# Softmax with a relative position bias: the first reload waits for one store instead of one and a half, and the engines' code stands without a block around it

## The chip, the cores and the metric

The kernel runs on one core of a Trainium2 chip. The metric is the device time of one execution in microseconds (us), the median of several executions of one build. The granted clock was 1.00 in every run, and no TensorE work is done.

Each profile covers one execution. Its "span" is 1.6 to 2.4 us shorter than the time that the metric gives for the same execution.

## The reference

```python
B, H, S = (2, 8, 2112)          # logits (B, H, S, S), rel_bias (H, 33), float32
rel = pos[:, None] - pos[None, :]
bias = rel_bias[:, np.clip(rel, -16, 16) + 16]
logits = logits + bias[None]
logits = logits - logits.max(axis=-1, keepdims=True)
exp = np.exp(logits)
return exp / exp.sum(axis=-1, keepdims=True)
```

285 MB are read once and 285 MB are written once.

## The kernel before

The 33,792 rows are spread over 128 partitions. A tile is R = 4 rows on each partition, 4224 KB. There are N = 66 tiles and BUFS = 6 buffers. VectorE adds the bias in place, ScalarE does the exponential with the row sums, VectorE scales. SyncE issues the stores and two short first loads; GpSimd issues the other loads. A reload of a buffer waits until the store out of it has landed. In the code, `take` waits until a semaphore (a counter that engines and transfers raise) has reached a value, and subtracts that value; `half` is the semaphore of the first half of the second store. The `nc.Block` holds one stream of instructions for each engine.

```python
    section = ctx.enter_context(tc.tile_critical(name="rows"))        # line 76
    ...
    def take(eng, sem, v):
        eng.wait_ge(sem, v).then_inc(sem, -v)

    def load(eng, u, start):
        eng.dma_start(out=L[u][:], in_=rows(logits, start)).then_inc(loaded[u], 16)

    def store(eng, u, start):
        take(eng, scaled, 1)
        eng.dma_start(out=rows(out, start), in_=L[u][:]).then_inc(stored[u], 16)

    def reload(eng, u, start):
        take(eng, stored[u], 16)
        load(eng, u, start)
    ...
    with nc.Block() as block:                                         # line 217

        @block.sync
        def _(eng):
            ...                                                       # first rows
            store(eng, 0, 0)
            take(eng, scaled, 1)
            for r0, r1, sem in ((0, R // 2, half), (R // 2, R, stored[1])):
                eng.dma_start(
                    out=rows(out, R + r0, (r1 - r0) * S), in_=L[1][:, r0 * S : r1 * S]
                ).then_inc(sem, 16)
            for n in range(2, BUFS):
                store(eng, n, n * R)
            passes(eng, BUFS, lambda u, start, loads: store(eng, u, start))
            for n in range(BUFS):
                take(eng, stored[n], 16)

        @block.gpsimd
        def _(eng):
            ...                                                       # first loads
            take(eng, half, 16)
            passes(eng, BUFS, lambda u, start, loads: reload(eng, u, start))
        ...                                                           # scalar, vector
```

The softmax here doesn't subtract the row's maximum and nothing guards it: scores larger than these inputs give would overflow.

Of the kernel before, what the change touches and what calls it, by code (L numbers as in the profile page):

```python
# [7 lines left out]
FP32 = mybir.dt.float32  # L8
INT32 = mybir.dt.int32
EXP = mybir.ActivationFunctionType.Exp  # L10
# [4 lines left out]
def kernel(  # L15
# [16 lines left out]





    nc = tc.nc
    P = 128
    B, H, S, S2 = logits.shape
# [4 lines left out]
    T = S // Q  # L44
    assert Q * B * H == P and T * Q == S and T % W == 0
    M = T // W
    R = 4
    PARTS = [(0, 2), (2, R)]
    BUFS = 6
    N = T // R  # L50
    assert N * R == T and N % BUFS == 0
    FW = S + T - 1
    NB = (FW - 2 * MR) // W
    assert NB * W + 2 * MR == FW
# [5 lines left out]
    one = const.tile([P, 1], FP32, tag="one", name="one")  # L60
    L = [const.tile([P, RS], FP32, tag=f"L{u}", name=f"L{u}") for u in range(BUFS)]
# [3 lines left out]
    qi, mm, qm, eq, lt, gt, rest = (  # L65
        L[BUFS - 1][:, NB * m : NB * (m + 1)] for m in range(7)
    )
    qi = qi.bitcast(INT32)
    mm = mm.bitcast(INT32)

    def rows(t, start, run=RS):
        return bass.AP(
            tensor=t.tensor, offset=t.offset + start * S, ap=[[T * S, P], [1, run]]
        )

    section = ctx.enter_context(tc.tile_critical(name="rows"))
    loaded = [nc.alloc_semaphore(f"loaded{u}") for u in range(BUFS)]
    stored = [nc.alloc_semaphore(f"stored{u}") for u in range(BUFS)]
    table = nc.alloc_semaphore("table")
    blocks_ready = nc.alloc_semaphore("blocks_ready")  # L80
    strip = nc.alloc_semaphore("strip")
    first = nc.alloc_semaphore("first")
    half = nc.alloc_semaphore("half")
    made = nc.alloc_semaphore("made")
    added = nc.alloc_semaphore("added")
    summed = nc.alloc_semaphore("summed")
# [1 line left out]
    scaled = nc.alloc_semaphore("scaled")  # L88
# [14 lines that stand above are left out]
# [16 lines left out]
    def exps(eng, u):  # L119
        for r0, r1 in PARTS:  # L120
            take(eng, added, 1)
            for i in range(r0, r1):
                x = L[u][:, i * S : (i + 1) * S]
                e = eng.activation(out=x, in_=x, func=EXP, accum_out=tot[u][:, i : i + 1])  # L124
            e.then_inc(summed, 1)

    def vec(eng, u, start, loads):
        eng.wait_ge(loaded[u], loads)
        for r0, r1 in PARTS:
            add(eng, u, r0, r1, start)  # L130
        for r0, r1 in PARTS:
            take(eng, summed, 1)
            t = tot[u][:, r0:r1]
            eng.reciprocal(out=t, in_=t).then_inc(inverted, 1)  # L134
            take(eng, inverted, 1)
            for i in range(r0, r1):
                x = L[u][:, i * S : (i + 1) * S]
                e = eng.tensor_scalar_mul(out=x, in0=x, scalar1=tot[u][:, i : i + 1])  # L138
        e.then_inc(scaled, 1)

    def passes(eng, n0, body):

        with eng.Fori(0, ((N - n0) // BUFS - 1) * 8 + 1, 8) as i:  # L143
            for n in range(n0, n0 + BUFS):
                body(n % BUFS, i * (BUFS * R // 8) + n * R, i * 2 + 16 * (n // BUFS + 1))
# [4 lines left out]
    def strip_of(eng):  # L150

        assert M * Q & (M * Q - 1) == 0
        low = rbP[:, W - 1 : W]
        high = rbP[:, 0:1]
        pitch = list(F.ap[0])[0]
        blocks = bass.AP(tensor=F.tensor, offset=F.offset + MR, ap=[[pitch, P], [W, NB], [1, W]])
        rev = bass.AP(
            tensor=rbP.tensor,
            offset=rbP.offset + W - 1,
            ap=[[list(rbP.ap[0])[0], P], [0, NB], [-1, W]],  # L160
        )

        def wide(t):
            return bass.AP(
                tensor=t.tensor, offset=t.offset, ap=[[list(t.ap[0])[0], P], [1, NB], [0, W]]
            )

        def step(ins):
            ins.then_inc(strip, 1)
            take(eng, strip, 1)  # L170

        take(eng, blocks_ready, 2)
        step(eng.tensor_single_scalar(out=qi, in_=qi, scalar=M * Q - 1, op=ALU.bitwise_and))  # L173
        step(eng.tensor_tensor(out=qm, in0=qi, in1=mm, op=ALU.subtract))  # L174
        for m, op in ((eq, ALU.is_equal), (lt, ALU.is_gt), (gt, ALU.is_lt)):
            step(eng.tensor_scalar(out=m, in0=qm, scalar1=0.0, scalar2=None, op0=op))  # L176
        take(eng, table, 16 * B)
        step(eng.tensor_scalar(out=rest, in0=lt, scalar1=low, scalar2=None, op0=ALU.mult))  # L178
        step(eng.tensor_copy(out=F[:, 0:MR], in_=low.to_broadcast([P, MR])))  # L179
        step(  # L180
            eng.scalar_tensor_tensor(  # L181
                out=rest, in0=gt, scalar=high, in1=rest, op0=ALU.mult, op1=ALU.add
            )
        )
        step(eng.tensor_copy(out=F[:, FW - MR : FW], in_=high.to_broadcast([P, MR])))  # L185
        step(eng.tensor_tensor(out=blocks, in0=wide(eq), in1=rev, op=ALU.mult))  # L186
        step(eng.tensor_tensor(out=blocks, in0=blocks, in1=wide(rest), op=ALU.add))  # L187
        eng.sem_inc(made, 1)

    def table_load(eng, bs):  # L190
        for b in bs:
            eng.dma_start(
                out=rbP[b * H * Q : (b + 1) * H * Q],
                in_=bass.AP(
                    tensor=rel_bias.tensor,
                    offset=rel_bias.offset,
                    ap=[[W, H], [0, Q], [1, W]],
                ),
            ).then_inc(table, 16)

    def row_load(eng, r0, m, sem):

        x = L[0]
        eng.dma_start(  # L204
            out=bass.AP(
                tensor=x.tensor,
                offset=x.offset + r0 * S,
                ap=[[list(x.ap[0])[0], P], [2 * S, m], [1, S]],
            ),
            in_=bass.AP(  # L210
                tensor=logits.tensor,
                offset=logits.offset + r0 * S,
                ap=[[T * S, P], [2 * S, m], [1, S]],
            ),
        ).then_inc(sem, 16)

    with nc.Block() as block:  # L217

        @block.sync
        def _(eng):  # L220

            row_load(eng, 0, 2, first)
            if R > 3:
                row_load(eng, 1, (R - 2) // 2, first)
            eng.wait_ge(loaded[BUFS - 2], 16)
            store(eng, 0, 0)
            take(eng, scaled, 1)
            for r0, r1, sem in ((0, R // 2, half), (R // 2, R, stored[1])):
                eng.dma_start(
                    out=rows(out, R + r0, (r1 - r0) * S), in_=L[1][:, r0 * S : r1 * S]  # L230
                ).then_inc(sem, 16)
            for n in range(2, BUFS):
                store(eng, n, n * R)
            passes(eng, BUFS, lambda u, start, loads: store(eng, u, start))
            for n in range(BUFS):
                take(eng, stored[n], 16)

        @block.gpsimd
        def _(eng):
            row_load(eng, R - 1 if R > 3 else 1, 1, loaded[0])  # L240
            eng.iota(qi, pattern=[[0, NB]], base=0, channel_multiplier=M).then_inc(  # L241
                blocks_ready, 1
            )
            eng.iota(mm, pattern=[[1, NB]], base=1 - M, channel_multiplier=0).then_inc(  # L244
                blocks_ready, 1
            )
            for n in range(1, BUFS):
                if n == BUFS - 1:
                    take(eng, made, 1)
                load(eng, n, n * R)  # L250
            take(eng, half, 16)
            passes(eng, BUFS, lambda u, start, loads: reload(eng, u, start))

        @block.scalar
        def _(eng):
            table_load(eng, range(B))


            eng.activation(  # L259
                out=one, in_=nc.const_aps.tensor(0.0, [P, 1], FP32), func=EXP  # L260
            )
            passes(eng, 0, lambda u, start, loads: exps(eng, u))

        @block.vector
        def _(eng):
            strip_of(eng)
            take(eng, first, 16 * (R - 2))
            passes(eng, 0, lambda u, start, loads: vec(eng, u, start, loads))


# [28 lines left out]
```

## Time and profile before

| | kernel before |
|---|---|
| time, median of 3 | 1328.84 us (1328.65 to 1331.46) |
| profiled execution | 1332.11 us, span 1330.3 us |
| moved | 570.99 MB, 433 GB/s in the steady stretch |
| busy | VectorE 72%, ScalarE 40%, both DMA queues together 99.7% |

### The profile page before, as it was taken

The numbers are of one execution on the slowest core, as the hardware profiler recorded it, in microseconds if no ns is written. First come the engines' busy times: TensorE is split into PE (matmuls) and PEld (weight loads), VectorE is DVE, ScalarE is ACT, GpSimd is POOL, SyncE is SP. The second block draws the span as 40 slices with busy tenths as digits, with TensorE's granted clock in tenths as the row PEclk, the third lists the DMA queues.
The fourth block names the chain that finished last, engine by engine and source line by source line (L and its number), as shares of the span: only waits on it lengthen the run. The fifth ranks groups of instructions, "written<-read, shape, count | busy, mean of one in ns | idle before, by whom it ended". The sixth has DMA issues, their size and how long they took to land. (4 is left out here: it accounts for less than half of the span.)

```text
span 1330.3 us, 2515 instructions
## 1 busy us (share of the span) xinstructions
DVE 954.2 (72%) x539; ACT 529.8 (40%) x530; POOL 37.1 (3%) x72
## 2 busy tenths in 40 slices
DVE  2888888677677677676676776776776776776771
ACT  0444445442442442442442442443443433433431
POOL 0000000000000000000000000000000000000000
DMA  9999999999999999999999999999999999999997
GB/s 394 430 417 431 435 431 434 436 428 437 433 430 437 434 428 438 434 429 437 435 429 435 435 429 436 433 432 435 431 434 435 430 436 434 429 437 434 429 436 337
DMA packets 19714, 570.99 MB, mean 429 GB/s; under 512 B 2304, under 2 KB 2304, under 8 KB 2304
## 3 DMA queue, kind: packets, MB, share of 16 engines
q1 hardware_dynamic: 10064, 288.72, 50.4%
q0 software_dynamic: 9504, 282.24, 49.3%
q10 hardware_dynamic: 144, 0.02, 0.0%
q14 instruction: 2, 0.02, 0.0%
HBM read 285.49 MB, written 285.47 MB: 429 GB/s over the span
## 5 line engine op out<-in xcount | busy, mean ns | idle before, releaser
L124 ACT ACTIVATE L<-L 128x2112 f32<-128x2112 f32 x264 | 516.0, 1955 | 768.4 <-ACTq L91 768.4
L117 DVE TENSOR_TENSOR L<-L,F 128x4224 f32<-128x4224 f32 x132 | 595.7, 4554 | 204.3 <-DMA L<-in_logits_dram 203.5
L138 DVE TENSOR_SCALAR L<-L,tot 128x2112 f32<-128x2112 f32 x264 | 336.4, 1316 | 21.4 <-DVEq L91 6.9
L134 DVE RECIPROCAL tot<-tot 128x2 f32<-128x2 f32 x132 | 21.4, 162 | 98.8 <-DVEq L91 98.8
L94 POOL DMA_DIRECT2D L<-in_logits_dram x65 | 36.0, 554 | 1212.8 <-POOLq L91 1212.8
L124 ACT ACTIVATION_READ_ACCUMULATOR L<-L 128x1 f32 x264 | 49.2, 186 | 0.0
L178 DVE TENSOR_SCALAR L<-L,rbP 128x71 f32<-128x71 f32 x1 | 0.3, 258 | 21.2 <-DVEq L91 21.2
L186 DVE TENSOR_TENSOR F<-L,rbP 128x2343 f32<-128x2343 f32 x1 | 2.6, 2601 | 0.1
L187 DVE TENSOR_TENSOR F<-F,L 128x2343 f32<-128x2343 f32 x1 | 2.6, 2600 | 0.1
L259 ACT ACT_TABLE_LOAD x1 | 1.3, 1283 | 2.9 <-issue 2.9
L173 DVE TENSOR_SCALAR L<-L 128x71 int32<-128x71 int32 x1 | 0.2, 198 | 2.9 <-DVEq L91 2.9
L176 DVE TENSOR_SCALAR L<-L 128x71 f32<-128x71 f32 x3 | 0.7, 239 | 0.4
L204 POOL DMA_DIRECT2D L<-in_logits_dram x1 | 0.7, 662 | 1.1 <-PEq L217 1.1
L181 DVE SCALAR_TENSOR_TENSOR L<-L,rbP 128x71 f32<-128x71 f32 x1 | 0.3, 296 | 0.2 <-DVEq L91 0.2
L174 DVE TENSOR_TENSOR L<-L 128x71 f32<-128x71 int32 x1 | 0.2, 234 | 0.1
L185 DVE COPY F<-rbP 128x16 f32<-128x16 f32 x1 | 0.2, 176 | 0.1
L179 DVE COPY F<-rbP 128x16 f32<-128x16 f32 x1 | 0.2, 175 | 0.1
L241 POOL IOTA L<- 128x71 int32 x1 | 0.2, 206 | 0.1
L259 ACT ACTIVATE one<-const-float32-0.0 128x1 f32<-128x1 f32 x1 | 0.2, 203 | 0.0
L244 POOL IOTA L<- 128x71 int32 x1 | 0.2, 207 | 0.0
L283 POOL MEMSET const-float32-0.0<- 128x1 f32 x1 | 0.1, 98 | 0.4 <-issue 0.4
L283 POOL MEMSET const-bfloat16-1.0<- 128x1 bf16 x1 | 0.1, 101 | 0.0
(2 smaller groups left out, 0.2 us busy)
## 6 DMA issues: line engine op xcount, KB each, us to landing
L<-in_logits_dram POOLq DMA_DIRECT2D x65, 4224.0 KB, 36.8
out_dram<-L SPq DMA_DIRECT2D x65, 4224.0 KB, 65.9
out_dram<-L SPq DMA_DIRECT2D x2, 2112.0 KB, 17.0
L<-in_logits_dram SPq DMA_DIRECT2D x1, 2112.0 KB, 10.5
L<-in_logits_dram SPq DMA_DIRECT2D x1, 1056.0 KB, 23.9
L<-in_logits_dram POOLq DMA_DIRECT2D x1, 1056.0 KB, 10.4
rbP<-in_rel_bias_dram ACTq DMA_DIRECT2D x2, 8.2 KB
```

What stands on the lines that cost most here:

```text
L94: eng.dma_start(out=L[u][:], in_=rows(logits, start)).then_inc(loaded[u], 16)
L117: eng.tensor_tensor(out=x3, in0=x3, in1=F3, op=ALU.add).then_inc(added, 1)
L124: e = eng.activation(out=x, in_=x, func=EXP, accum_out=tot[u][:, i : i + 1])
L134: eng.reciprocal(out=t, in_=t).then_inc(inverted, 1)
L138: e = eng.tensor_scalar_mul(out=x, in0=x, scalar1=tot[u][:, i : i + 1])
L176: step(eng.tensor_scalar(out=m, in0=qm, scalar1=0.0, scalar2=None, op0=op))
L178: step(eng.tensor_scalar(out=rest, in0=lt, scalar1=low, scalar2=None, op0=ALU.mult))
L181: eng.scalar_tensor_tensor(out=rest, in0=gt, scalar=high, in1=rest, op0=ALU.mult, op1=ALU.add)
L186: step(eng.tensor_tensor(out=blocks, in0=wide(eq), in1=rev, op=ALU.mult))
L187: step(eng.tensor_tensor(out=blocks, in0=blocks, in1=wide(rest), op=ALU.add))
L204: eng.dma_start(out=bass.AP(tensor=x.tensor, offset=x.offset + r0 * S, ap=[[list(x.ap[0])[0], P], [2 * S, m], [1, S]],), in_=bass.AP(tenso ...
L259: eng.activation(out=one, in_=nc.const_aps.tensor(0.0, [P, 1], FP32), func=EXP)
```

## The change

The intent is a simpler start and a simpler frame: the first reload goes out as soon as its own buffer is free, the second store is one transfer like all others, and the four engines' instruction streams are written without a block around them.

```diff
-    half = nc.alloc_semaphore("half")
...
-    with nc.Block() as block:
-        @block.sync
-        def _(eng):
...
-            store(eng, 0, 0)
-            take(eng, scaled, 1)
-            for r0, r1, sem in ((0, R // 2, half), (R // 2, R, stored[1])):
-                eng.dma_start(
-                    out=rows(out, R + r0, (r1 - r0) * S), in_=L[1][:, r0 * S : r1 * S]
-                ).then_inc(sem, 16)
-            for n in range(2, BUFS):
-                store(eng, n, n * R)
-            passes(eng, BUFS, lambda u, start, loads: store(eng, u, start))
+    def sync_part(eng):
...
+        passes(eng, 0, lambda u, start, loads: store(eng, u, start))
...
-            take(eng, half, 16)
-            passes(eng, BUFS, lambda u, start, loads: reload(eng, u, start))
+        passes(eng, BUFS, lambda u, start, loads: reload(eng, u, start))
...
+    sync_part(nc.sync)
+    gpsimd_part(nc.gpsimd)
+    scalar_part(nc.scalar)
+    vector_part(nc.vector)
```

The first row loads keep their sizes, although they are written differently.

More of the change, by code (lines that the diff above doesn't have):

```diff
@@ L50 @@
     N = T // R
-    assert N * R == T and N % BUFS == 0
+    assert N * R == T and N % BUFS == 0 and R % 2 == 0
     FW = S + T - 1
@@ L215, in row_load @@
         ).then_inc(sem, 16)
-    with nc.Block() as block:
-        @block.sync
-        def _(eng):
-            row_load(eng, 0, 2, first)
-            if R > 3:
-                row_load(eng, 1, (R - 2) // 2, first)
-            eng.wait_ge(loaded[BUFS - 2], 16)
-            store(eng, 0, 0)
-            take(eng, scaled, 1)
-            for r0, r1, sem in ((0, R // 2, half), (R // 2, R, stored[1])):
-                eng.dma_start(
-                    out=rows(out, R + r0, (r1 - r0) * S), in_=L[1][:, r0 * S : r1 * S]
-                ).then_inc(sem, 16)
-            for n in range(2, BUFS):
-                store(eng, n, n * R)
-            passes(eng, BUFS, lambda u, start, loads: store(eng, u, start))
-            for n in range(BUFS):
-                take(eng, stored[n], 16)
-        @block.gpsimd
-        def _(eng):
-            row_load(eng, R - 1 if R > 3 else 1, 1, loaded[0])
-            eng.iota(qi, pattern=[[0, NB]], base=0, channel_multiplier=M).then_inc(
-                blocks_ready, 1
-            )
-            eng.iota(mm, pattern=[[1, NB]], base=1 - M, channel_multiplier=0).then_inc(
-                blocks_ready, 1
-            )
-            for n in range(1, BUFS):
-                if n == BUFS - 1:
-                    take(eng, made, 1)
-                load(eng, n, n * R)
-            take(eng, half, 16)
-            passes(eng, BUFS, lambda u, start, loads: reload(eng, u, start))
-        @block.scalar
-        def _(eng):
-            table_load(eng, range(B))
-            eng.activation(
-                out=one, in_=nc.const_aps.tensor(0.0, [P, 1], FP32), func=EXP
-            )
-            passes(eng, 0, lambda u, start, loads: exps(eng, u))
-        @block.vector
-        def _(eng):
-            strip_of(eng)
-            take(eng, first, 16 * (R - 2))
-            passes(eng, 0, lambda u, start, loads: vec(eng, u, start, loads))
@@ new lines, in sync_part, with gpsimd_part @@
+    def sync_part(eng):
+        row_load(eng, 0, R // 2, first)
+        row_load(eng, 1, R // 2 - 1, first)
+        eng.wait_ge(loaded[BUFS - 2], 16)
+        passes(eng, 0, lambda u, start, loads: store(eng, u, start))
+        for n in range(BUFS):
+            take(eng, stored[n], 16)
+    def gpsimd_part(eng):
+        row_load(eng, R - 1, 1, loaded[0])
+        eng.iota(qi, pattern=[[0, NB]], base=0, channel_multiplier=M).then_inc(
+            blocks_ready, 1
+        )
+        eng.iota(mm, pattern=[[1, NB]], base=1 - M, channel_multiplier=0).then_inc(
+            blocks_ready, 1
+        )
+        for n in range(1, BUFS):
+            if n == BUFS - 1:
+                take(eng, made, 1)
+            load(eng, n, n * R)
+        passes(eng, BUFS, lambda u, start, loads: reload(eng, u, start))
@@ L272, with scalar_part, vector_part @@
+    def scalar_part(eng):
+        table_load(eng, range(B))
+        eng.activation(
+            out=one, in_=nc.const_aps.tensor(0.0, [P, 1], FP32), func=EXP
+        )
+        passes(eng, 0, lambda u, start, loads: exps(eng, u))
+    def vector_part(eng):
+        strip_of(eng)
+        take(eng, first, 32)
+        passes(eng, 0, lambda u, start, loads: vec(eng, u, start, loads))
+    sync_part(nc.sync)
+    gpsimd_part(nc.gpsimd)
+    scalar_part(nc.scalar)
+    vector_part(nc.vector)
 _INS = ['logits', 'rel_bias']
```

## The prediction

> **What bounds the kernel now.** I read the page from its second part downwards: first the DMA rows, then the queue table, then the groups with their idle times, then the order of issues between 55 and 90 us, because that is the only stretch that the change touches, and last the closing instructions.
>
> ```profile
> DVE 954.2 (72%) x539; ACT 529.8 (40%) x530; POOL 37.1 (3%) x72
> ...
> DMA  9999999999999999999999999999999999999997
> ...
> DMA packets 19714, 570.99 MB, mean 429 GB/s; under 512 B 2304, under 2 KB 2304, under 8 KB 2304
> ...
> q1 hardware_dynamic: 10064, 288.72, 50.4%
> q0 software_dynamic: 9504, 282.24, 49.3%
> ```
>
> The two rows of the queue table add up to 99.7% of what 16 DMA engines can spend in the span. q0 carries the loads that GpSimd issues, q1 the stores (and two short first loads) that SyncE issues. No compute engine is near that: VectorE has 72%. So transfers bound the kernel almost from end to end.
>
> ```profile
> L117 DVE TENSOR_TENSOR L<-L,F 128x4224 f32<-128x4224 f32 x132 | 595.7, 4554 | 204.3 <-DMA L<-in_logits_dram 203.5
> ...
> L94 POOL DMA_DIRECT2D L<-in_logits_dram x65 | 36.0, 554 | 1212.8 <-POOLq L91 1212.8
> ...
> L<-in_logits_dram POOLq DMA_DIRECT2D x65, 4224.0 KB, 36.8
> out_dram<-L SPq DMA_DIRECT2D x65, 4224.0 KB, 65.9
> ```
>
> The first line says that VectorE's only large wait (203.5 us) is for loads. The second says that GpSimd waits almost all the time for stores to land, which is how a saturated ring of six buffers looks: there is nothing to reload into until a store is out. The last two say that a tile's load takes 36.8 us and its store 65.9 us from issue to landing. One tile is 4224 KB = 4.325 MB, which at the steady 433 GB/s (the window from 400 to 700 us) is 10.0 us of all 16 engines. So a load is issued while nearly one more is in front of it, and a store waits behind several. 36.8 + 65.9 + some 16 us of compute = 119 us, six buffers times the 20 us that one load and one store take. The queues hold the slack; the compute does not.
>
> **How far it is from its floor.** In the trace's packet records a full packet is 33,792 B and takes 1.251 us, in steady state almost without exception. There are 132 tile transfers (66 in, 66 out), 8 such packets each for each of 16 engines: 1056 x 1.251 = 1321.1 us. The first packet starts at 2.2 us of the span, so an engine that never idles ends at 1323.3. Fifteen engines end between 1322.6 and 1325.0 us, that is, they have next to no idle time to give. One ends at 1328.5: the last of a store's 16 ends trails the eighth by 1.6 us for the first store, 3.3 us near 130 us, and 5.4 us for the last. From load 7 to load 65 that engine needs 20.06 us for each load and store where the others need 19.97: it loses some 0.1 us per tile. SyncE's last wait ends just after it (1328.9), and barriers and drains take the rest to 1330.3. All that could be won by perfect queueing is therefore about 5 us of 1330, or 0.4%, and nearly all of it belongs to that one slow engine.
>
> **What the Trainium skill says.** (1) "DMA: Bandwidth & Descriptors", section "Where 436 GB/s comes from", puts the ceiling of the 16 ports at 435.2 GB/s; the trace's 433 GB/s agrees, so there is no faster rate for a new order of transfers to find. (2) The same page, "Issuing engines are not separate DMA queues": transfers issued by different engines share the same 16 DMA engines and interleave; the trace agrees (both queues together 99.7%), so starting a load earlier takes its bandwidth from a store. (3) Its table "Latency and other measured facts" says that DMA engines 7 and 15 are usually slower than the rest and offers descriptor-ring contention as an unsure cause. The one slow engine here fits that; the records don't number the engines, so which it is isn't shown.
>
> **The change, part by part.** It (a) removes GpSimd's wait for the first half of the second store, (b) sends the second store as one transfer of 4224 KB in place of two of 2112 KB, (c) takes the first six stores into the loop, and (d) drops the block around the engines' code. The three-row first loads keep their sizes: R is 4, so two rows, one row, one row as before.
>
> ```profile
> 55.67 0.35 SPq L98 DMA_DIRECT2D out_dram<-L  x1
> ...
> 66.23 1.84 SPq L229 DMA_DIRECT2D out_dram<-L  x2
> ...
> 81.89 0.53 POOL L94 DMA_DIRECT2D L<-in_logits_dram  x1 [47.94 <-POOLq L91]
> ...
> 82.29 64.82 SPq L98 DMA_DIRECT2D out_dram<-L  x5
> 86.61 0.53 POOL L94 DMA_DIRECT2D L<-in_logits_dram  x1 [4.19 <-POOLq L91]
> ```
>
> (a) The first store's last packet ends at 75.5 us in the records, the first half of the second store's at 80.5, the second half's at 85.6. The second reload is issued 86.61 - 85.6 = 1.0 us after its store's last packet. So without the half the first reload should be issued at 75.5 + 1.0 = 76.5 us, 5.4 us before the 81.89 of now. What does this fill? From 76 to 82 us the DMA is busy with store 1 alone already (422 GB/s), so the earlier load only shares those 6 us. It may fill one hole: in the windows
>
> ```profile
> 82.00:84.00 2.00, 2.00 (x2) 0.00 (x0) 0.42 (x1) 1.00 1.31 482
> 84.00:86.00 2.00, 2.00 (x1) 0.00 (x0) 0.00 (x0) 1.00 0.82 253
> ```
>
> the rate (last column) averages (482 + 253) / 2 = 367 GB/s over 4 us, against 433: (1 - 367/433) x 4 = 0.6 us of lost transfer, where store 1 has run out, its reload is just starting and store 2 has only been issued. With the load under way from 78 us, store 1 would last until about 91 and store 2 would wait behind it, so this hole should close; but the start of a load beside a running store may make a like dip of its own (store 0 starting beside load 5 did, near 59 us). I count half: -0.3 us.
>
> Afterwards the phase differs. Now two reloads start within 4.7 us and run nearly as a pair for the rest of the kernel; after the change the second reload waits for store 1, which now shares, until about 92 us, while load 0 needs until about 98. So some 1.3 loads instead of 1.84 will be outstanding, and by the same sum of 119 us the stores' time should grow: **about 26 us for a load and 77 for a store**. The total of the two is fixed by six buffers and 20 us per tile. The bytes are the same.
>
> (b) One SyncE issue less, of 0.4 us or so on an engine that waits nearly always: 0. (c) A few register operations per store on SyncE: 0. (d) The block's end costs the drain and the barrier from 1328.97 to 1329.14 us, after the last store: -0.2 us, on the path. At its entry no gain: ScalarE issues its first transfer 0.1 us after its branch and SyncE likewise.
>
> Sum: -0.3 - 0.2 = -0.5 us, 1328.84 -> **1328.3 us**.
>
> **The rivals.** First, the load queue could run dry between reloads, as only 1.3 would be outstanding, and that engines start each load with a delay. Load k+1 would be issued some 5 us before load k ends and take 1.9 us to its first packet (81.89 to 83.8 for the first one now), which leaves 3 us; the slow engine's lag reaches 5 us towards the end, so the other 15 may find q0 empty for a while. Against a loss speaks that several stores wait in q1 throughout, so they take stores meanwhile. If the slow engine itself lost 0.05 us more per load, that would be 60 x 0.05 = +3 us. Second, the earlier load delays the second store, and with it all reloads by 5 us or so, and VectorE starves at the end: then the last load would land later than 1288.0 us, and the last compute (16 us) plus the last store (10 us) would stick out. Now the DMA has 1328.5 - 1288 = 40 us of stores left at that moment, of which 27 are needed; even 10 us less would be hidden. With fewer loads outstanding the last load should even land earlier, near 1283. Third, the slow engine's lag is partly made in the start, and a smoother start takes 1 to 2 us off the end: one engine seems to stand idle for 1.9 us near 86 us; but the engine that ends last gains its lag over the whole run, so I give this little weight. Fourth, the half had been put in because it won something: the sums show no more than a microsecond or two.
>
> **Range and chances.** The three runs of before lie within 2.8 us (1328.65 to 1331.46), the rivals within +3 and -2. I take 1325.5 to 1331.5 as the 80% range. 2% would be 26.6 us, five times all that can be won and far above any loss I can construct while both queues have work: 1% for each side.
>
> **What would show it right or wrong.** Right: first reload issued near 76.5 us; no dip under 400 GB/s in 84 to 86; load landing near 26 us and store near 77; DMA share still over 99%; last packet of the slow engine within 2 us of 1328.5; VectorE's wait for loads still about 200 us. Wrong: a steady rate under 430 GB/s, a gap of several microseconds without packets, a last load later than 1295 us, or a slow engine whose lag grows by other than 0.1 us per tile.

## The result

| | before | changed |
|---|---|---|
| time, median of 4 | 1328.76 us (1328.65 to 1331.46) | 1335.37 us (1335.23 to 1335.76) |
| span of the profiled execution | 1330.3 us | 1333.3 us |
| load, store: issue to landing | 36.8, 65.9 us | 31.8, 71.0 us |
| VectorE's wait for loads | 203.5 us | 200.2 us |
| last packet of the last store ends | 1328.5 us | 1326.4 us |

The ratio is 1.0045, with a 95% interval of 1.0028 to 1.0063. A ratio here is worked out from the runs of both kernels and not from their medians, so it is not quite the ratio of the medians. Executions over 1.5% slower than the fastest of the same kernel are left out of the means. The change is slower by 6.6 us in the medians. That is "the same" by a 2% rule, but it is far outside the noise of this kernel and outside the predicted range.

The last row of the table is the odd one. The transfers end earlier, in the profiled executions, and yet the span is longer. First the page of the changed kernel, for what has not changed:

```profile
DVE 954.7 (72%) x539; ACT 529.8 (40%) x530; POOL 37.0 (3%) x72
...
DMA packets 19571, 570.99 MB, mean 428 GB/s; under 512 B 2289, under 2 KB 2289, under 8 KB 2289
...
L114 DVE TENSOR_TENSOR L<-L,F 128x4224 f32<-128x4224 f32 x132 | 595.7, 4554 | 201.0 <-DMA L<-in_logits_dram 200.2
...
out_dram<-L SPq DMA_DIRECT2D x66, 4224.0 KB, 71.0
L<-in_logits_dram POOLq DMA_DIRECT2D x65, 4224.0 KB, 31.8
```

The compute groups and the bytes are those of before. Only the times in the queues have moved, some 5 us from loads to stores. Next, the end of the changed kernel by windows of 2 us (columns: window, length, busy time of VectorE, ScalarE and GpSimd, clock, DMA share, GB/s):

```profile
1320.00:1322.00 2.00, 0.00 (x0) 0.00 (x0) 0.00 (x0) 1.00 0.90 389
1322.00:1324.00 2.00, 0.00 (x0) 0.00 (x0) 0.00 (x0) 1.00 0.08 34
1324.00:1326.00 2.00, 0.00 (x0) 0.00 (x0) 0.00 (x0) 1.00 0.04 17
1326.00:1328.00 2.00, 0.00 (x0) 0.00 (x0) 0.00 (x0) 1.00 0.00 0
```

From 1322 us on about one DMA engine of 16 is at work, and after 1326.4 us none is. Nothing computes and nothing moves for the 7 us that follow. The waits of SyncE's sequencer say what it stands for. These are the three longest in the changed kernel:

```profile
SPq L88 <- SPq L88: 1234.3, 68, 19.7
SPq L140 <- DMA L<-in_logits_dram: 52.3, 1, 52.3
SPq L74 <- POOLq L74: 5.3, 1, 5.3
```

The first two are the ordinary waits for tiles. The third is new: 5.3 us, once, at line 74, for GpSimd. Line 74 opens the critical section (line 76 in the kernel before), and its closing instructions carry that line. The view of that line (engine, operation, count, duration in ns as least/median/most, first and last start) shows the instruction:

```profile
L74 ACTq DRAIN  x1: 13/13/13, 1327.0 to 1327.0; - x1
L74 POOLq DRAIN  x1: 5446/5446/5446, 1327.0 to 1327.0; - x1
L74 DVEq DRAIN  x1: 17/17/17, 1327.0 to 1327.0; - x1
```

A DRAIN is an instruction of its own in the trace, and the engine does nothing else until it ends. ScalarE and VectorE are through with theirs in under 20 ns, but GpSimd takes 5446 ns. In the kernel before the same line and the block's line read

```profile
L76 POOLq DRAIN  x1: 47/47/47, 1329.2 to 1329.2; - x1
```

```profile
L217 POOLq DRAIN  x1: 39403/39403/39403, 1251.1 to 1251.1; - x1
```

The block ended with a drain on each engine, as soon as that engine was through with its own code. GpSimd got there at 1251.1 us, right after its last load was issued, and drained until 1290.5 us. Its last load had landed at 1287.7 us. The stores ran on until 1328.5 us, so this cost nothing, and the section's own drain then took 47 ns. Without the block there is no early drain, and the whole of it falls after the last store.

### The profile page after: what moved, and what is told of

It reads as the page before. It is cut to its first block, busy times and chain, and to the rows that moved or that the text cites. A ratio compares the mean times of both kernels' runs of the same rounds, so it can differ in the third digit from the quotient of the medians.

```text
span 1333.3 us, 2515 instructions
## 1 busy us (share of the span) xinstructions
DVE 954.7 (72%) x539; ACT 529.8 (40%) x530; POOL 37.0 (3%) x72
## 5 line engine op out<-in xcount | busy, mean ns | idle before, releaser
L114 DVE TENSOR_TENSOR L<-L,F 128x4224 f32<-128x4224 f32 x132 | 595.7, 4554 | 201.0 <-DMA L<-in_logits_dram 200.2
L241 ACT ACT_TABLE_LOAD x1 | 1.3, 1283 | 2.9 <-issue 2.9
## 6 DMA issues: line engine op xcount, KB each, us to landing
L<-in_logits_dram POOLq DMA_DIRECT2D x65, 4224.0 KB, 31.8
```

Of the source, the lines that this page charges most:

```text
L114: eng.tensor_tensor(out=x3, in0=x3, in1=F3, op=ALU.add).then_inc(added, 1)
L241: eng.activation(out=one, in_=nc.const_aps.tensor(0.0, [P, 1], FP32), func=EXP)
```

## The experiments

The theory after this reading, A, was that the lost early drain accounts for 5.4 us. The rival, B, was that the new order of transfers costs the 6.6 us, through the slow DMA engine. Each run was timed in turn with the kernel before on the same chip; the differences below are between medians of one job.

**The block put back, all else as changed.**

```diff
-    sync_part(nc.sync)
-    gpsimd_part(nc.gpsimd)
...
+    with nc.Block() as block:
+        block.sync(sync_part)
+        block.gpsimd(gpsimd_part)
...
```

> The changed kernel with the block put back around the engines' code; the shorter wait and the unsplit second store stay. Theory A (GpSimd's drain of 5.4 us, which the block had let run while transfers went on, now stands after the last store): about 1335.4 - 5.4 + 0.2 = 1330.2 us, and a long GpSimd drain that starts near 1251 us, right after its last load, with none over 0.1 us after the last store. Rival B (the shorter wait costs the 6.6 us by a worse order of transfers): stays at 1335 us.

It took 1330.77 us, beside 1328.95 for the kernel before: +1.8 us (ratio 1.0013, 1.0000 to 1.0027). The section's GpSimd drain is down to 47 ns, and a drain of 34.5 us stands at the block's line from 1251.2 us on, as expected:

```profile
L74 POOLq DRAIN  x1: 47/47/47, 1327.0 to 1327.0; - x1
```

**The block taken away, all else as before.** The `with` line and the decorators go, the four bodies become functions, and the waits and the split store stay.

> The kernel before with only its block taken away; the wait for half of the second store and the split store stay. Theory A: 1328.8 + 5.4 - 0.2 = about 1334.0 us, with a drain of GpSimd of about 5.4 us as the last long instruction after the last store. Rival B: 1328.6 us, no change but the barrier.

It took 1334.34 us: +5.4 us over the kernel before (ratio 1.0038, 1.0024 to 1.0052). The drain is back at the end in this kernel, with the wait for the half still there:

```profile
L76 POOLq DRAIN  x1: 5451/5451/5451, 1325.8 to 1325.8; - x1
```

These two runs rule out B as the main cause. The block alone carries 5.4 us.

**One drain added to the changed kernel.**

```diff
         passes(eng, BUFS, lambda u, start, loads: reload(eng, u, start))
+        eng.drain()
```

> The changed kernel with one GpSimd drain added straight after its last load, and no block. Theory A: about 1335.4 - 5.4 = 1330.0 us, the drain at the end under 0.1 us, the added one hidden from about 1251 us to a few us after the last load has landed. Rival B: 1335 us. If the drain at the end still takes 5 us, the drain is not a cost of earlier loads but of the place, and theory A needs mending.

It took 1330.45 us (+1.5). The added drain lasts 34.5 us and is hidden, and the one at the end is 47 ns:

```profile
L236 POOLq DRAIN  x1: 34489/34489/34489, 1251.7 to 1251.7; - x1
```

```profile
L74 POOLq DRAIN  x1: 47/47/47, 1327.4 to 1327.4; - x1
```

So the block as such is not needed: one instruction in the right place does the same. In the runs with an early drain, and in the kernel before, that drain ended 2.2 to 3.2 us after the last load had landed, with more than 30 us of stores still to come.

**What the drain costs by the number of loads.** The reload loop is cut in two, with the drain between the parts, so that 12 loads follow it.

```diff
-        passes(eng, BUFS, lambda u, start, loads: reload(eng, u, start))
+        half(0, K - 2)            # K = 10 passes over the six buffers
+        eng.drain()
+        half(K - 2, K)
```

> The changed kernel with a GpSimd drain before its last 12 reloads, so that only 12 loads of 65 follow it. If the drain at the end costs in proportion to the loads since the last drain, it takes 5.4 x 12/65 = 1.0 us there and the run is 4.4 us shorter than the changed kernel, unless the drain in the middle (which holds reloads back by some 20 us once) is not hidden by the stores that wait. If its cost is fixed once there is any load, it stays at 5.4 us.

The drain at the end took 1034 ns, against the 1.0 us expected:

```profile
L74 POOLq DRAIN  x1: 1034/1034/1034, 1327.3 to 1327.3; - x1
```

A drain with no transfer since the one before took 47 ns here. Less that, it is (1034 - 47) / 12 = 82 ns for each of 12 transfers, and (5446 - 47) / 66 = 82 ns for each of the 66 that GpSimd issues in the changed kernel. The cost grows with the transfers issued since the last drain, even when all of them have landed long ago: the last load landed at about 1283 us, 44 us before the drain at the end of the changed kernel began. Whether it goes by transfers or by bytes is not shown, as all but one are of 4224 KB. The run took 1330.8 us, so the reloads that the drain in the middle held back cost nothing that shows.

Theory A was right, but the kernels with the early drain and the short wait were still 1.5 to 1.9 us over the kernel before, where I had expected 0.5 us under it. The next question was whether the block's absence or the new order costs this.

**The kernel before, no block, with the early drain.** As the second run above, with the added drain of the third.

> The kernel before without its block (wait for the half and split store kept), with one GpSimd drain added after its last load. If the block matters only through that drain: the kernel before less a barrier, 0 to 0.3 us under it, some 1328.7 us, and 1.5 us under the changed kernel with the same drain (1330.45). If the block's absence costs something else too, it stays above the kernel before by that.

It took 1327.75 us, beside 1328.43 for the kernel before: -0.7 us (ratio 0.9994, 0.9981 to 1.0007). No other cost of the block's absence shows. So the order of transfers was left.

**The changed kernel with the early drain and a longer wait.**

```diff
+        eng.wait_ge(stored[1], 16)
         passes(eng, BUFS, lambda u, start, loads: reload(eng, u, start))
+        eng.drain()
```

> The changed kernel with the early GpSimd drain, whose first reload waits for the whole second store as well; the store stays one transfer. Theory C (the 1.5 us that the drain leaves over come from the order of transfers, through how many loads are outstanding: two reloads that start as a pair cost the slow DMA engine less than reloads spaced evenly): loads take about 37 us again and the run about 1329 us. Rival D (they come from the second store's being one transfer, or are noise of the chip): stays at 1330.5 us.

It took 1329.21 us (+0.8; ratio 1.0000, 0.9987 to 1.0013), with one run of six slow (1350.16), which is left out of the ratio; the median of the five fast runs is 1329.18. Loads took 47.4 us from issue to landing, more than the 37 expected. It lies between the two others, too close to both for a verdict. For that reason all three were run again on one chip, with a fourth that separates the wait from the split of the store.

**Short wait, unsplit store, early drain (again).**

> Second sight, for a comparison on one chip, of the changed kernel with the early GpSimd drain (the first reload waits for the first store only, the second store is one transfer). If the shorter wait costs something of its own, it is 1 to 2 us over the kernel before and 2 us or more over the next one here; if the 1.5 us of the first time came of the chip or of chance, all four lie within 1 us.

**Wait for the half, split store, early drain (again).**

> Second sight of the kernel before without its block and with the early drain (wait for the half, split store): 0.2 to 0.7 us under the kernel before, as the first time.

**Short wait, split store, early drain.** Only the second reload waits for both halves.

```diff
+        reload(eng, 0, BUFS * R)
         take(eng, half, 16)
-        passes(eng, BUFS, lambda u, start, loads: reload(eng, u, start))
+        for n in range(1, BUFS):
+            reload(eng, n, (BUFS + n) * R)
+        passes(eng, 2 * BUFS, lambda u, start, loads: reload(eng, u, start))
```

> As the one above (early drain, no block, second store split in two), but the first reload no longer waits for the half; only the second reload waits for both halves. Theory C (the wait, through the order of transfers that it sets): as the first kernel here, 1 to 2 us over the kernel before, loads near 32 us. Rival D (the split of the store is what helps): as the second one here, under the kernel before.

**Wait for the whole second store, unsplit, early drain (again).**

> Second sight of the first kernel here with a first reload that also waits for the whole second store, sent as one. Theory C: near the second one here, at most 1 us over it. Rival D: near the first one here.

| first reload waits for | second store | median | over before (1328.68) | ratio, 95% |
|---|---|---|---|---|
| first store | whole | 1330.53 us | +1.9 | 1.0014 (1.0001 to 1.0027) |
| first store | split | 1330.53 us | +1.9 | 1.0016 (1.0003 to 1.0029) |
| and half of the second | split | 1328.01 us | -0.7 | 0.9998 (0.9985 to 1.0011) |
| and all of the second | whole | 1329.60 us | +0.9 | 1.0025 (0.9999 to 1.0052) |

In the last row, one execution of six took 1341.38 us; it pulls the ratio, not the median. The first two rows agree to the hundredth, so with the short wait the split does not help. The second against the third, which differ in the wait alone, is 2.5 us between medians and 2.2 us between means: that is what the wait for the half is worth in this job. The two kernels' runs overlap a little (1329.38 to 1333.25 against 1327.68 to 1330.00). With the first sight of the kernels of rows one and three it was 1330.45 - 1327.75 = 2.7 us, across two jobs. The last row waits longest and gains only 0.9 us, so a longer wait is not simply better.

The packet records show where it sits. In every profile, one of the 16 DMA engines ends later than the 15 others. The table gives, for the last store, when the middle of the 16 ends and when the last does, and how much the engine that is last at load 65 fell further behind the middle since load 30, by the ends of the loads. (The records do not number the engines, but it can be followed, since the others keep their distance. In three of the kernels another engine was still behind it at load 30.)

| kernel | middle ends | last ends | lag gained by that engine, load 30 to 65 |
|---|---|---|---|
| changed | 1321.9 | 1326.4 | 2.9 us |
| changed, block back | 1321.9 | 1326.2 | 2.9 us |
| changed, early drain | 1322.0, again 1321.8 | 1326.8, 1326.5 | 2.9, 2.9 us |
| same, split store | 1321.9 | 1327.3 | 3.3 us |
| half waited for, no block | 1322.7 | 1325.3 | 0.8 us |
| half waited for, early drain | 1321.8, again 1322.2 | 1324.2, 1325.6 | 1.0, 1.9 us |
| whole second store waited for | 1322.2, again 1321.9 | 1325.8, 1325.2 | 2.4, 1.9 us |
| before (a long execution) | 1323.1 | 1328.5 | 3.2 us |

In all five profiles with the short wait the slow engine loses about 2.9 us or more there, and the last packet ends at 1326.2 us or later; in all five profiles with a longer wait, apart from the kernel before's own, it loses at most 2.4 us, and the last packet ends at 1325.8 us or earlier. The profiled execution of the kernel before, 1332.11 us, is the exception. Its other executions lay between 1327.7 and 1331.5 us, so that kernel too seems to fall into the worse pattern at times; its other executions left no packet records to check that. The idea of theory C, that it goes by how many loads are outstanding, is not borne out: a load takes 36.8 us from issue to landing in the kernel before and in the same kernel without its block, and the slow engine loses 3.2 us in the one and 0.8 us in the other; where a load takes 47.4 us it loses 2.4 us. (The run with the drain in mid-stream also has the short wait, but holds its reloads back near 1011 us, and is left out of the table.) What in the interleaving makes the slow engine lose more per tile is open: I looked for packets that took longer than 1.251 us, and found no point in the period of a tile at which the excess gathers.

**All loads from SyncE.** To see whether the slow engine and the drain both belong to GpSimd's transfers, all loads were issued by SyncE, in one queue with the stores (reload n + 6, then store n + 4).

> All loads and reloads issued by SyncE in one queue with the stores, none by GpSimd; no block. The drain at the end should then cost under 0.1 us with no drain added, as GpSimd has no transfers. If the slow DMA engine (4 to 5 us behind the rest at the end) comes of GpSimd's descriptors, all 16 engines end within 1.5 us of each other and the run takes about 1322.5 + 1 + 1.9 = 1325.5 us; if it is a slow engine whatever the queue, 1329 to 1330 us. One queue in order may also lose time in the start, where loads wait behind stores: up to +5 us.

It took 1332.52 us (+4.1; ratio 1.0026, 1.0013 to 1.0039). The drain at the end is short, with none added:

```profile
L74 POOLq DRAIN  x1: 41/41/41, 1329.7 to 1329.7; - x1
```

Fifteen engines ended within 0.2 us of each other (1326.4 to 1326.6), but one still ended at 1329.2. The 2.6 us between them are what was left after the others had stood idle near the end (below): at the last store but one the last engine was 6.9 us behind the middle one, and six more were 1.1 to 4.6 us behind. So a slow engine is there without any GpSimd transfer, and its lag is no smaller. This version lost time at the end:

```profile
1300.00:1310.00 10.00, 9.85 (x5) 5.59 (x5) 0.00 (x0) 1.00 1.00 433
1310.00:1320.00 10.00, 3.78 (x4) 2.42 (x4) 0.00 (x0) 1.00 0.66 281
```

The DMA runs at 281 GB/s for these 10 us, (1 - 281/433) x 10 = 3.5 us lost, while the last tile is still being computed: with a shorter store backlog (33.4 us from issue to landing) the last tile's compute seems no longer covered.

No version beat the kernel before clearly. The closest is the kernel before with its block replaced by the one early drain, -0.7 us in each of two jobs, with both intervals across 1, so a gain is not shown.

## Why the prediction was wrong

**What bounds the kernel:** right. The rate in the stretch from 400 to 700 us is 433 GB/s in both kernels, VectorE's wait for loads is about 200 us in both, and the first reload was issued at 76.05 us (predicted 76.5). The next steps that the text gave as tests came out mixed. Loads and stores took 31.8 and 71.0 us instead of 26 and 77; the direction was right, and the size was half. The rate from 84 to 86 us was 355 GB/s, not over 400, so a dip stayed. The last load let VectorE begin at 1283.4 us, as predicted (near 1283). The slow engine's last packet ended at 1326.4 us, 2.1 us before the 1328.5 (within 2 us was the test); it lost 2.9 us in 35 loads, 0.08 us for each, near the 0.1 that the prediction named.

**Part (d), the block's end, is the step that failed.** The prediction priced it as "the drain and the barrier from 1328.97 to 1329.14 us, after the last store: -0.2 us". It looked at the block's closing only where it was on the path, and did not ask what the block had moved off the path. GpSimd's 39.4 us drain at line 217 stood in the trace of the kernel before, 79 us ahead of the span's end. With the block gone, 5446 ns of it reappeared after the last store. Taking only the block away cost 5.4 us; adding one drain gave it back. Against the kernel before, the changed kernel was at +6.6 us; with the block back it was at +1.8 and with the one drain at +1.5.

**The first rival's slow engine, and the sign of part (a), failed by a smaller amount.** The prediction counted -0.3 us for the earlier reload, and allowed "+3 us" if the slow engine lost 0.05 us more per load. A cost of that size came about: the short wait cost 2.5 us against the same kernel with the wait, seen as a slow engine that falls back by 2.9 us or more over 35 loads instead of 0.8 to 2.4. Whether it comes of a load queue that runs dry, as the rival has it, is not shown. The middle engines ended no later with the short wait (1321.8 to 1322.0 us, against 1321.8 to 1322.7 in the other profiles without the kernel before's); the end is set by the last engine. The prediction read the slow engine's rate in a profile that was itself an exception (3.2 us over the 35 loads), so it could not see there that the longer wait can do better. The fourth rival, that the half had been put in because it won something, was put at "no more than a microsecond or two", and it is worth about 2.

The terms add up to: -0.7 (block away, early drain kept, two jobs) + 2.5 (short wait) + 5.4 (drain at the end) = +7.2 us, against +6.6 measured; the terms come from different jobs, and the difference is within the spread of the executions. The range of 1325.5 to 1331.5 would have held the 1330.5 us of the changed kernel with an early drain. It missed by the drain.

## What to carry to other kernels

When a change removes a frame (a block, a section, a barrier), read every instruction that carries the frame's line in the trace, on all engines and at all times, also those that are far from the end and hidden: what is hidden today because of where it stands can be exposed tomorrow. In a kernel whose GpSimd issues many transfers, let GpSimd drain as soon as it has issued its last one, while stores still run; here that one instruction was worth 5 us of 1335. Where DMA is saturated, judge an order of transfers by the last of the 16 engines, not by their mean rate: the rate was 433 GB/s before and after.

## What the Trainium skill lacked or had wrong

- "VectorE: DVE Perf Modes", section "The DRAIN you can't avoid", says that the drains of the preamble and postamble take about 12 ns on all five engines. At the start and the end of the program of the kernel before, ScalarE, VectorE, SyncE and TensorE come near that (7 to 10 ns), but GpSimd's took 34 to 182 ns. The section has no drain like the one that closes the kernel's own section, where GpSimd's took 5446 ns when it had issued 66 transfers since its last drain, 1034 ns for 12, and 41 to 47 ns for none.
- No page has that a GpSimd drain costs some 82 ns for each transfer that GpSimd issued since the one before, after all of them have landed. It would belong to "DMA: Bandwidth & Descriptors", beside the cost of issuing from GpSimd.
- "DMA: Bandwidth & Descriptors", table "Latency and other measured facts", calls the slowness of DMA engines 7 and 15, in a best guess that it marks as not certain, specific to transfers issued by GpSimd. With no such transfer at all, the last engine was 6.9 us behind the middle one at the last store but one, and ended 2.6 us after the fifteen others (1329.2 against at most 1326.6 us); with them the last ended 2.4 to 5.4 us after the middle one. The records don't number the engines, so whether it is one of those two is not shown.
